# Two causal pooling layers: token means as TensorE products with a constant matrix, from token-major inputs in the first layer and from a token-major first product in the last

## The chip, the cores and the metric

The kernel runs on one core of one Trainium2 chip. The metric is the device time of one execution in microseconds (us). Times are the median of repeated runs; rows come from one execution that was recorded by the hardware profiler.

## The reference

One step of a decoder trunk with four layers on T = 264 tokens: a prompt of 256 new tokens, and 8 further sequences with one new token each and a state of their own. The model is 1024 wide. Layers 0 and 3 mix the tokens by pooling, layer 1 by a gated delta rule, layer 2 by retention, and a SwiGLU network (FFN) follows each. Every sublayer ends in a layer norm of `alpha * x + sublayer(x)`. The pooling mixer, cut to what matters:

```python
for gi, win in enumerate((2, 4, 8, 16)):       # four groups of 256 features
    lo, hi = gi * 256, (gi + 1) * 256
    s = c[:, 16:16 + T, lo:hi] - c[:, 16 - win:16 - win + T, lo:hi]   # c: running sum of [buffer, x]
    cnt = jnp.minimum(t + 1 + n_valid, win)
    means.append(s / cnt[None, :, None])
pooled = jnp.concatenate(means, axis=-1) - x
out = einsum('btgc,gcd->btgd', pooled by group, w) * scale
return out, ext[:, -15:]                        # and the last 15 input rows as the new state
```

For the 8 sample tokens the window reaches into `state_pool`, 15 earlier rows for each sequence.

## The kernel before

Activations lie feature-major: `x` is [128 partitions, 8 blocks, 264 tokens]. Every weight product is made of three fp32r products (`mm3`): both operands are split in a high part that fp32r holds exactly and the rest, and high by high, high by low and low by high are summed in PSUM. Weights come on SP's queue in 1 MB chunks (`raw`, a ring of three). ACT casts the high part in pieces of 128x512 (L205, `h`) and DVE subtracts it for the low part (L206, `l`); for the pooling weights POOL does the latter. So a chunk of weights needs a landing, casts on ACT and subtractions on DVE before TensorE can start with it.

A scheduler sets the order of the instructions, by its own model of their times, and each engine then runs its queue strictly in that order; `keep_in_program_order` pins single ones. An instruction that waits holds up all that stand behind it on its engine.

Layer norms of class `LN` come in two kinds. A deferred one hands its successor the unnormalised `d` times the gain, split in `zh` and `zl`. The next product is made from these, and mean and scale are put in later, when its results leave PSUM (`unfold`); x itself is made along the way by `apply`. One that is not deferred ends with `stats` and `finish`: sums on TensorE against a constant 1/1024, then mean `mr`, variance `vv`, `r` = 1/sqrt by Ln and Exp on ACT (L364, L365) and a Newton step on DVE (L366 to L368), then x by blocks. In before, the norm behind FFN 2 is of the second kind.

A pooling layer (`pool_layer`) takes x and makes the window sums by doubling shifts: adds of 128x510 elements and the like on DVE, for the group of window 16 on POOL (L545 to L560), and copies of the edges on ACT. `ph` and `pl` are the halves of the result (L561, L562) for 12 products per block of 128 outputs. L571 adds the product to `ax`, which is alpha times x. The mean `c` of the first two blocks (L331) is subtracted from all blocks before they are summed (L297, and on POOL L565 for groups 1 to 3). `busy` issues bf16 products with a constant tile `ob` that compute nothing; `BUSY` holds how many.

In an FFN the gate phase makes 22 pairs of products with `w13`, each followed by Silu on ACT (L456), a product on DVE (L457, `s`) and the split `gh` (L458) and `gl`. The down phase reads `w2` in chunks of 16 products, 11 chunks. Ahead of it a table of functions with Ln and Exp is loaded in ACT (L477), since Silu has another one. During FFN 2 the retention states are brought up to date: `st` and `vbc` are loaded, 1 MB each, and `out_ret_s` stored.

Of the kernel before, what the change touches and what calls it, by code (L numbers as in the profile page):

```python
# [19 lines left out]
P = 128  # L20
# [16 lines left out]

BUSY = ((20, 4), (44, 4))

# [21 lines left out]
CL, CN = _const_layout()  # L61
VL, VN = {}, 0
for _n, _c in (("psc", 16), ("lng", 64), ("lnb", 64), ("ng", 1), ("cw", 96), ("alog", 8), ("dtb", 8), ("corr", 128)):
    VL[_n] = (VN, _c)
    VN += _c


def make_consts():
# [33 lines left out]
    for h in range(H):  # L102
# [4 lines left out]
        dec[h, :, TP:] = d0[:, :P]  # L107
    return c.astype(np.float32), rope.astype(np.float32), dec.astype(np.float32), lev


@with_exitstack
def body(ctx: ExitStack, tc: tile.TileContext, ap):
# [156 lines left out]
    class LN:  # L269
# [5 lines left out]

        def __init__(self, idx, defer, on_pe=False):
            self.idx, self.defer, self.on_pe = idx, defer, on_pe
            self.c, self.seen = None, []
            self.d = pers.tile([P, KB, T], F32, tag="d", name=nm("d"))
            if on_pe:  # L280
                self.p1, self.p2 = sm_ps([P, T]), sm_ps([P, T])
            else:
                self.s1 = lnp.tile([P, T], F32, tag="s1", name=nm("s1"))
                self.s2 = lnp.tile([P, T], F32, tag="s2", name=nm("s2"))
            if defer:
                self.zh = pers.tile([P, KB, T + 2], F32R, tag="xz", name=nm("zh"), bufs=2)
                self.zl = pers.tile([P, KB, T + 2], F32R, tag="xz", name=nm("zl"), bufs=2)
                G.tensor_copy(self.zh[:, :, T:T + 2], gbh[:, idx])
                G.tensor_copy(self.zl[:, :, T:T + 2], gbl[:, idx])
# [53 lines left out]

        def stats(self):
            if self.on_pe:
# [40 lines left out]

        def apply(self, m):
# [5 lines left out]
            G.tensor_tensor(x[:, m], y, u, ADD)  # L393
            S.copy(xh[:, m], x[:, m])  # L394
            V.tensor_tensor(xl[:, m], x[:, m], xh[:, m].bitcast(F32), SUB)  # L395
# [51 lines left out]
    def ffn(l, pln):  # L447
        with tc.tile_pool(name=f"ffn{l}", bufs=1) as fp:
# [12 lines left out]
            for j in range(FB):  # L461
# [37 lines left out]

    def pool_layer(l, j, _):  # L500
        with tc.tile_pool(name=f"pool{l}", bufs=1) as pp:
            st = pp.tile([P, KB, NB, 15], F32, name=nm("st"))
            ob = pp.tile([P, 512], BF16, name=nm("ob"))
# [7 lines left out]
            busy(BUSY[l > 0][0])  # L511
            raw = wp.tile([P, CW], F32, tag="raw", name=nm("raw"))
            if l == 0:
                tc.keep_in_program_order(S.preload_act_table_set("natural_log_exp_and_others"))
            for g in range(4):
                w = slice(2 * g, 2 * g + 2)
                if l == 0:
                    nc.sync.dma_start(x[:, w], ap["xT"][:, w])
                    if g == 0:
                        nc.scalar.dma_start(vec, ap["vec"])  # L520
# [4 lines left out]
            if l == 0:  # L525
                small_loads()
            hl = [split(raw[:, i * 1024:(i + 1) * 1024], 1024, wp, "w", G) for i in range(2)]
            ss = pp.tile([P, KB, NB], F32, name=nm("ss"))
# [3 lines left out]
            co = W("corr", 0, 128).rearrange("p (b t) -> p b t", b=KB)  # L532
            ln = LN(l * 2, True, True)
            if l:
                tc.keep_in_program_order(S.preload_act_table_set("natural_log_exp_and_others"))
            for g in range(4):
                b0 = 2 * g
                win = 2 << g
                xb = x[:, b0:b0 + 2]
                E = G if g == 3 else V  # L540
                if g == 0:

                    dst = pp.tile([P, 2, T], F32, tag="s0", name=nm("sw"), bufs=2)
                    sc = 0.5
                    V.tensor_tensor(dst[:, :, 1:TP], xb[:, :, 0:TP - 1], xb[:, :, 1:TP], SUB)  # L545
                    G.tensor_tensor(dst[:, :, 0:1], xb[:, :, 0:1], xb[:, :, 0:1], SUB)
                    G.tensor_tensor(dst[:, :, TP:T], st[:, b0:b0 + 2, :, 14], xb[:, :, TP:T], SUB)
                else:
                    sc = 1.0
                    src = xb  # L550
                    for i in range(g + 1):
                        sh = 1 << i
                        dst = pp.tile([P, 2, T], F32, tag=f"s{g % 2}", name=nm("sw"), bufs=2)
                        E.tensor_tensor(dst[:, :, sh:TP], src[:, :, sh:TP], src[:, :, 0:TP - sh], ADD)
                        S.copy(dst[:, :, 0:sh], src[:, :, 0:sh])
# [20 lines left out]
                if g < 3:  # L576
                    busy(BUSY[l > 0][1])
            nc.scalar.dma_start(ap["pool_o"][j], st)
            tl = pp.tile([P, KB, 15 + NB], F32, name=nm("tl"))
            G.tensor_copy(tl, x[:, :, TP - 15:T])  # L580
            nc.scalar.dma_start(ap["pool_t"][j], tl)
            return ln
# [732 lines left out]
    "y": (P, KB, T),  # L1315
    "pool_o": (2, P, KB, NB, 15),
    "pool_t": (2, P, KB, 15 + NB),
# [9 lines left out]
def prepare(inp):  # L1327
# [24 lines left out]
    ch = lambda w: w.reshape(w.shape[:-1] + (w.shape[-1] // P, P))  # L1352
    corr = np.zeros((KB, 16))
    for b in range(KB):
        win = (2, 4, 8, 16)[b // 2]
        corr[b] = win / np.minimum(np.arange(16) + 1, win)
    vecs = [
# [6 lines left out]
        np.broadcast_to(a["gdn_dt_bias"][0], (P, 8)),  # L1364
        np.broadcast_to(corr.astype(np.float32).reshape(1, KB * 16), (P, KB * 16)),
    ]
    o["vec"] = con(np.concatenate(vecs, 1))
    o["cst"], o["rope"], o["rdec"], o["lev"] = make_consts()
    return o


def unpack(r):
    y = np.asarray(r["y"]).transpose(2, 1, 0).reshape(T, 1024)
    pt = np.asarray(r["pool_t"]).transpose(0, 3, 2, 1).reshape(2, 15 + NB, 1024)
    po = np.asarray(r["pool_o"]).transpose(0, 3, 4, 2, 1).reshape(2, NB, 15, 1024)
    pp = pt[:, None, :15]
# [27 lines left out]
```

## Time and profile before

| what | value |
|---|---|
| median of 3 runs | 1396.97 us (1396.32 to 1398.08) |
| the profiled execution's own time | 1399.02 us |
| its span, first to last instruction | 1397.2 us |
| mean granted TensorE clock | 0.978 of full speed |
| TensorE busy | 1326.9 us (95%) |
| VectorE (DVE) busy | 1044.3 us (75%) |
| ScalarE (ACT) busy | 841.8 us (60%) |
| GpSimd (POOL) busy | 460.2 us (33%) |

The time of the profiled execution lies 1.8 us above its span, and 2.05 us above the median of the other runs. TensorE's share is an average: it works without a break in the FFNs and waits at the two pooling layers and at a few other places.

### The profile page before, as it was taken

What the parts mean: (1) busy time and instruction counts of PE and PEld (TensorE: products, weight loads), DVE (VectorE), ACT (ScalarE), POOL (GpSimd) and SP (SyncE); (2) the same over time, 40 slices, a digit from 0 to 9 for tenths busy, and PEclk for the clock granted to TensorE, in tenths of its full rate; (3) what the DMA queues carried; (4) which work ended last, traced back from release to release, by engine and by line L of the source; (5) the groups of instructions that cost most, each with busy time, mean ns of one, the idle gap of its engine ahead of it and who ended that gap; (6) DMA issues with size and microseconds to landing.
All of it is one profiled execution on the core that took longest, in us unless ns stands there. A gap on an engine that the chain in (4) does not pass through costs nothing. (4 is left out here: it accounts for less than half of the span.)

```text
span 1397.2 us, 27688 instructions
## 1 busy us (share of the span) xinstructions
PE 1326.9 (95%) x10506; PEld 1273.5 (91%) x10509; DVE 1044.3 (75%) x2075; ACT 841.8 (60%) x1971; POOL 460.2 (33%) x518
## 2 busy tenths in 40 slices
PE   6999999879999999999979999999999998999996
PEld 4999999778998999999979999999998995999996
DVE  8885566989666799777697777668976758975564
ACT  4774544658564677675566665557765654774543
POOL 5230013563353443001278664133300144330022
PEclk8999999889999999999989999999999999999998
DMA  6355555421323355895645554456589961355550
GB/s 230 121 183 181 181 174 185 151 90 63 105 77 110 132 211 184 305 325 210 235 148 181 197 195 137 150 181 271 182 343 388 347 212 67 132 201 182 181 178 35
DMA packets 44341, 257.06 MB, mean 184 GB/s; under 512 B 5040, under 2 KB 9776, under 8 KB 16560
## 3 DMA queue, kind: packets, MB, share of 16 engines
q1 hardware_dynamic: 35936, 223.17, 44.9%
q10 hardware_dynamic: 5968, 19.55, 3.9%
q0 software_dynamic: 2304, 12.58, 2.2%
q8 instruction: 82, 1.34, 0.4%
q14 instruction: 51, 0.42, 0.1%
HBM read 238.45 MB, written 16.84 MB: 183 GB/s over the span
## 5 line engine op out<-in xcount | busy, mean ns | idle before, releaser
L206 DVE TENSOR_TENSOR l<-raw,h 128x512 fp32r<-128x512 f32 x658 | 463.1, 739 | 121.7 <-ACT h L205 116.9
L205 ACT CAST h<-raw 128x512 fp32r<-128x512 f32 x680 | 386.9, 616 | 193.9 <-PE mm L123 155.5
L123 PE MATMUL mm<-xh,h 128*128 128x264 f32 x1216 | 348.1, 288 | 8.2 <-ACT xh L394 4.0
L123 PE MATMUL mm<-xl,h 128*128 128x264 f32 x1216 | 348.4, 287 | 5.1 <-DVE xl L395 5.1
L123 PE MATMUL mm<-xh,l 128*128 128x264 f32 x1216 | 346.3, 287 | 0.0
L123 PEld LDWEIGHTS mm<-xh,h 128*128 128x128 f32 x1216 | 230.1, 190 | 10.8 <-ACT xh L394 4.8
L123 PEld LDWEIGHTS mm<-xl,h 128*128 128x128 f32 x1216 | 230.4, 189 | 5.9 <-DVE xl L395 5.3
L123 PEld LDWEIGHTS mm<-xh,l 128*128 128x128 f32 x1216 | 229.4, 189 | 0.7 <-DVE l L206 0.4
L123 PE MATMUL mm<-gh,l 128*128 128x264 f32 x704 | 199.6, 285 | 0.6 <-DVE l L206 0.6
L123 PE MATMUL mm<-gh,h 128*128 128x264 f32 x704 | 200.0, 284 | 0.0
L123 PE MATMUL mm<-gl,h 128*128 128x264 f32 x704 | 198.9, 283 | 0.0
L123 PE MATMUL mm<-zh,l 128*128 128x266 f32 x496 | 140.9, 289 | 3.0 <-DVE l L206 2.9
L123 PE MATMUL mm<-zh,h 128*128 128x266 f32 x496 | 142.1, 291 | 0.9 <-DVE ab L403 0.6
L123 PE MATMUL mm<-zl,h 128*128 128x266 f32 x496 | 142.5, 289 | 0.0
L123 PEld LDWEIGHTS mm<-gh,l 128*128 128x128 f32 x704 | 132.1, 188 | 1.0 <-DVE l L206 0.9
L123 PEld LDWEIGHTS mm<-gh,h 128*128 128x128 f32 x704 | 132.5, 188 | 0.1
L123 PEld LDWEIGHTS mm<-gl,h 128*128 128x128 f32 x704 | 132.5, 188 | 0.0
L404 POOL TENSOR_TENSOR ab<-ab,u 128x264 f32<-128x264 f32 x68 | 66.7, 992 | 138.5 <-DVE ab L403 59.6
L123 PE MATMUL mm<-xh,w 128*128 128x264 f32 x416 | 107.9, 314 | 2.1 <-DVE ab L403 2.1
L123 PEld LDWEIGHTS mm<-zh,l 128*128 128x128 f32 x496 | 92.9, 189 | 4.4 <-DVE l L206 4.1
L123 PEld LDWEIGHTS mm<-zh,h 128*128 128x128 f32 x496 | 93.1, 189 | 2.5 <-DVE ab L403 2.0
L123 PEld LDWEIGHTS mm<-zl,h 128*128 128x128 f32 x496 | 93.9, 189 | 1.0 <-DVE zl L300 0.2
(401 smaller groups left out, 2699.8 us busy)
## 6 DMA issues: line engine op xcount, KB each, us to landing
raw<-in_w_dram SPq DMA_DIRECT2D x132, 1024.0 KB
raw<-in_rwi_dram SPq DMA_DIRECT2D x24, 1024.0 KB
raw<-in_gwi_dram SPq DMA_DIRECT2D x16, 1024.0 KB
st<-in_rst_dram ACTq DMA_DIRECT2D x8, 1024.0 KB
raw<-in_rwo_dram SPq DMA_DIRECT2D x8, 1024.0 KB
st<-in_rst_dram SPq DMA_DIRECT2D x8, 1024.0 KB
vbc<-vdr SPq DMA_DIRECT2D x8, 1024.0 KB
out_ret_s_dram<-st POOLq DMA_DIRECT2D x8, 1024.0 KB, 10.6
```

The costliest lines, as they stand in the source:

```text
L123: i = nc.tensor.matmul(*a, **k)
L205: S.copy(hi[:, w], src_ap[:, w])
L206: (E or V).tensor_tensor(lo[:, w], src_ap[:, w], hi[:, w].bitcast(F32), SUB)
L404: (E or G).tensor_tensor(out, out, u[:n], ADD)
```

## The change

- **Layer 0.** Two new inputs: `xk`, the tokens of x and the pool state, token-major, 4 groups of [128, 3, 256] (393 KB each), and `pa`, constant matrices of means (128 x 4 x 296, 606 KB). `means` makes window mean minus x of one block by four fp32 products of 128, 16, 128 and 8 columns. The shifted adds, their edge copies and the correction table `corr` go away. `ph` and `pl` are made per block from PSUM. The pool state is stored from `xk` in four pieces, and no longer loaded as `st` (480 KB).
- **FFN 2.** The norm behind it is now deferred. `zh` and `zl` get 8 more columns, for the sums of the pool state of layer 3, which `pool_rows` loads ahead of `w2` in a slot of the ring `raw`.
- **Layer 3.** `pool_late` multiplies `zh` and `zl` with the pooling weights first, with tokens as the output's partitions (72 products of up to 256 columns into `zt` and `z3p`; four bf16 products with `zero` clear the banks). The statistics of the norm come behind that, a product with `m18` puts the mean in, `r` is turned to a column (`rc`), `zs` is `zt` times it, and `means` then makes the feature-major block. x is made by `apply` (L414 to L417 in the changed kernel). No `busy` and no load of a table are placed here.

```diff
-BUSY = ((20, 4), (44, 4))
+BUSY = (20, 4)
...
-            ln = LN(l * 2 + 1, l in (0, 1))
+            ln = LN(l * 2 + 1, l < DEPTH - 1, more=NB if l == 2 else 0)
+            if l == 2:
+                pool_rows(ln)
             tc.keep_in_program_order(S.preload_act_table_set("natural_log_exp_and_others"))
...
+    def pool_rows(ln):
+        st = wp.tile([P, CW], F32, tag="raw", name=nm("raw"))[:, 0:KB * NB * 15].rearrange("p (k b r) -> p k b r", k=KB, b=NB)
+        nc.sync.dma_start(st, ap["pst"])
+        nc.gpsimd.dma_start(ap["pool_o"], st)
...
+    def means(ps, rows, g, pa, n, o):
+        r0, r1, r2 = rows
+        PE.matmul(ps[:, P:TP], r1, pa[:, g, P:TP], start=True, stop=False)
+        PE.matmul(ps[:, P:P + 16], r0, pa[:, g, TP:TP + 16], start=False, stop=True)
+        PE.matmul(ps[:, 0:P], r0, pa[:, g, 0:P], start=True, stop=True)
+        PE.matmul(ps[:, TP:T], r2, o, start=True, stop=True)
...
+    def pool_late(l, j, pln):
...
+            for g in range(4):
...
+                PE.matmul(zt[g], zero[:, 0:P], zero, start=True, stop=False)
+                for c in (2, 0, 1):
...
+                    for kk in range(2):
+                        a, b = pln.zh[:, 2 * g + kk, w], pln.zl[:, 2 * g + kk, w]
+                        f = slice(kk * 256, kk * 256 + 256)
+                        PE.matmul(out, a, hi[:, f], start=c == 2 and kk == 0, stop=False)
+                        PE.matmul(out, b, hi[:, f], start=False, stop=False)
+                        PE.matmul(out, a, lo[:, f], start=False, stop=kk == 1 and c == 2)
+                S.copy(z3s[:, g], z3p[g // 2][:18, g % 2])
+            pln.stats(pa[:18, 3, 288:289])
...
+                for c in range(2):
+                    S.mul(zs[:, c], zt[g][:, c], rc[:, c:c + 1])
+                for m in (b0, b0 + 1):
+                    pln.apply(m, False)
...
+                    means(ps, (zs[:, 0, f], zs[:, 1, f], z3s[:, g, f]), g, pa, 18, a3[:, g])
+                    V.scalar_tensor_tensor(ln.d[:, m], ps[:, 0:T], W("psc", j * 8 + m), ax[:, m], MUL, ADD)
...
             for g in range(4):
-                nc.sync.dma_start(st[:, w], ap["pst"][j, :, w])
+                nc.sync.dma_start(xk[g], ap["xk"][g])
+                nc.scalar.dma_start(pa[:, g], ap["pa"][:, g])
...
+                    means(ps, (xk[g][:, 0, f], xk[g][:, 1, f], xk[g][:, 2, f]), g, pa, P, pa[:, g, 272:280])
+                    S.copy(ph[:, m], ps[:, 0:T])
+                    V.tensor_tensor(pl[:, m], ps[:, 0:T], ph[:, m].bitcast(F32), SUB)
...
+            for g in range(4):
+                nc.scalar.dma_start(ap["pool_k"][g], xk[g][:NB * 15, 2])
```

Three places in the order of the queues. The first is the head of ACT's queue, before; `raw_117` holds the pooling weights, and a wait names the semaphore that must have risen (DMAHW is a DMA).

```order
3 L524 DMA raw_117<-in_pw_dram 128x1024 x2
4 L170 DMA cst<-in_cst_dram 128x656
5 L174 DMA wba<-in_gba_dram 128x128 [waits DMAHW1_49]
6 L205 CAST h_143<-raw_117 128x512 [waits DMAHW3_49]
7 L205 CAST h_143<-raw_117 128x512
```

The same place of the changed kernel, where `raw_116` holds the pooling weights and `xk_119` to `xk_122` the four groups of `xk`:

```order
5 L645 DMA pa_118<-in_pa_dram 128x296
6 L645 DMA pa_118<-in_pa_dram 128x296 [waits DMAHW1_49]
7 L648 DMA raw_116<-in_pw_dram 128x1024 [waits DMAHW3_49]
8 L645 DMA pa_118<-in_pa_dram 128x296 [waits DMAHW5_49]
9 L191 DMA cst<-in_cst_dram 128x656 [waits DMAHW7_49]
10 L195 DMA wba<-in_gba_dram 128x128 [waits DMAHW0_49]
11 L226 CAST h_151<-raw_116 128x512 x2
```

The first cast has moved behind seven issues of transfers that each wait for an earlier one; DMAHW0 in row 10 is the landing of the third `xk`.

The second is ACT's queue where FFN 2 goes from its gate to its down phase, before. The last `s` is the Silu of the last gate pair, `raw_2227_14294` the first chunk of `w2`.

```order
1528 L205 CAST h_2228_14296<-raw_2227_14294 128x512 [waits DMAHW6_49,PE_49,Activation_49]
1529 L205 CAST h_2228_14296<-raw_2227_14294 128x512
1530 L205 CAST h_2230_14302<-raw_2227_14294 128x512 [waits DVE_49,PE_49]
1531 L205 CAST h_2230_14302<-raw_2227_14294 128x512
1532 L456 ACTIVATE s_2223_14278<-mm_2221_14228 128x264 [waits PE_49]
1533 L458 CAST gh_1961_12464<-s_2223_14278 128x264 [waits DVE_49]
```

The same place of the changed kernel, where `raw_2232_14323` is the first chunk of `w2`:

```order
1528 L538 CAST zh_2228_14308<-ss_2231_14315 128x8x8 [waits DVE_49]
1529 L505 ACT_TABLE_LOAD
1530 L482 ACT_TABLE_LOAD [waits PE_49]
1531 L482 ACTIVATE s_2224_14293<-mm_2222_14243 128x264 [waits Activation_49]
1532 L484 CAST gh_1962_12479<-s_2224_14293 128x264 [waits DVE_49]
1533 L226 CAST h_2233_14325<-raw_2232_14323 128x512 [waits DMAHW7_49]
```

The casts of the first chunk of `w2` have moved from ahead of the last Silu to behind it, and two loads of tables stand ahead of that Silu; in before the only one (L477) came 17 rows later.

The third is ACT's queue in layer 3 of the changed kernel, around the statistics of the norm (`sm_15208` is the sum of d):

```order
1612 L226 CAST h_15538<-raw_15536 128x512 [waits DMAHW0_49,PE_49,Pool_49]
1613 L226 CAST h_15538<-raw_15536 128x512
1614 L376 COPY mr_15212<-sm_15208 128x264 [waits PE_49]
1615 L381 ACTIVATE t_15216<-sm_15208 128x264
1616 L388 ACT_TABLE_LOAD
1617 L388 ACTIVATE r_15220<-vv_15218 128x264 [waits DVE_49]
1618 L389 ACT_TABLE_LOAD
1619 L389 ACTIVATE r_15220<-r_15220 128x264 [waits Activation_49]
```

In before the one load of this place (L535) stood ahead of the last products of FFN 2; now a load stands ahead of Ln and another ahead of Exp.

## Rows read from the trace of the kernel before

**Rows 1.** The page: busy us of each engine, share of the span, instructions.

```profile
PE 1326.9 (95%) x10506; PEld 1273.5 (91%) x10509; DVE 1044.3 (75%) x2075; ACT 841.8 (60%) x1971; POOL 460.2 (33%) x518
```

**Rows 2.** Busy time by engine, clock and DMA, three stretches of layer 0.

```profile
core 0: us, PE busy (x) PEld busy (x) DVE busy (x) ACT busy (x) POOL busy (x), PEclk, DMA share, GB/s
0.00:4.00 4.00, 2.53 (x6) 0.89 (x7) 0.56 (x2) 1.28 (x1) 0.19 (x4) 1.00 0.56 160
4.00:8.00 4.00, 3.79 (x15) 1.43 (x13) 1.30 (x6) 1.67 (x4) 2.43 (x6) 1.00 1.01 370
8.00:12.00 4.00, 1.92 (x12) 1.56 (x12) 3.99 (x7) 3.22 (x10) 4.00 (x5) 1.00 1.08 410
```

**Rows 3.** Timeline of layer 0, rows of ACT, DVE, POOL and PE (start, duration, instruction).

```profile
6.33 1.14 ACT L205 CAST h<-raw 128x512 fp32r<-128x512 f32 x2 [4.33 <-DMA raw<-in_pw_dram]
18.53 0.39 ACT L331 ACTIVATE c<-sm 128x264 f32<-128x264 f32 x1 [1.06 <-PE sm L123]
...
18.96 1.90 DVE L297 TENSOR_TENSOR d<-d,c 128x264 f32<-128x264 f32 x2
27.63 0.48 DVE L300 SCALAR_TENSOR_TENSOR zl<-d,vec,zh 128x264 fp32r<-128x264 f32 x1
28.03 1.28 DVE L206 TENSOR_TENSOR l<-raw,h 128x512 fp32r<-128x512 f32 x2
...
19.00 4.75 POOL L565 TENSOR_TENSOR ax<-ax,c 128x528 f32<-128x528 f32 x3 [2.02 <-ACT c L331]
...
35.30 0.60 PE L123 MATMUL mm<-ph,h 128*128 128x264 f32 x2
35.73 0.28 PE L123 MATMUL mm<-zh,h 128*128 128x266 f32 x1
35.85 0.29 PE L123 MATMUL mm<-zl,h 128*128 128x266 f32 x1
```

**Rows 4.** Timeline of ACT where FFN 2 turns from gate to down phase.

```profile
1082.32 0.39 ACT L456 ACTIVATE s<-mm 128x264 f32<-128x264 f32 x1 [1.56 <-PE mm L123]
1083.22 0.41 ACT L458 CAST gh<-s 128x264 fp32r<-128x264 f32 x1 [0.51 <-DVE s L457]
1083.54 1.14 ACT L205 CAST h<-raw 128x512 fp32r<-128x512 f32 x2
```

**Rows 5.** Timeline of ACT in FFN 3: a load of a table and the Silu behind it.

```profile
1199.84 1.28 ACT L456 ACT_TABLE_LOAD   x1
1201.13 0.43 ACT L456 ACTIVATE s<-ab 128x264 f32<-128x264 f32 x1
```

**Rows 6.** Timeline of PE in FFN 2: its longest wait there.

```profile
1057.52 0.39 PE L123 MATMUL mm<-xh,h 128*128 128x264 f32 x1 [2.64 <-ACT h L205]
```

**Rows 7.** Busy time, clock and DMA after that wait, and after one in layer 2.

```profile
1056.00:1058.00 2.00, 0.48 (x4) 0.48 (x4) 1.44 (x4) 1.47 (x4) 0.53 (x1) 1.00 1.00 422
...
720.00:722.00 2.00, 0.00 (x0) 0.00 (x0) 2.00 (x2) 1.94 (x6) 2.00 (x3) 1.00 0.00 0
728.00:732.00 4.00, 4.00 (x20) 4.00 (x20) 2.98 (x8) 0.69 (x2) 1.30 (x2) 0.50 0.27 53
```

**Rows 8.** Timeline from the end of FFN 2 to FFN 3, rows of four engines.

```profile
1147.95 1.05 PE L123 MATMUL sm<-s,cst 128*128 128x264 f32 x4
1148.84 0.61 PE L123 MATMUL sm<-d,cst 128*128 128x264 f32 x2
1150.61 9.44 PE L123 MATMUL sm<-ob 128*128 128x512 bf16 x43 [0.35 <-DMA st<-in_pst_dram]
...
1149.48 0.38 ACT L355 COPY mr<-sm 128x264 f32<-128x264 f32 x1
...
1155.08 0.86 DVE L368 SCALAR_TENSOR_TENSOR r<-t,r 128x264 f32<-128x264 f32 x1
...
1166.24 0.39 ACT L331 ACTIVATE c<-sm 128x264 f32<-128x264 f32 x1 [2.10 <-PE sm L123]
...
1182.94 0.59 PE L123 MATMUL mm<-ph,h 128*128 128x264 f32 x2
```

More of the change, by code (lines that the diff above doesn't have):

```diff
@@ L61 @@
 CL, CN = _const_layout()
+NPA = 296
 VL, VN = {}, 0
-for _n, _c in (("psc", 16), ("lng", 64), ("lnb", 64), ("ng", 1), ("cw", 96), ("alog", 8), ("dtb", 8), ("corr", 128)):
+for _n, _c in (("psc", 16), ("lng", 64), ("lnb", 64), ("ng", 1), ("cw", 96), ("alog", 8), ("dtb", 8)):
     VL[_n] = (VN, _c)
@@ L107, in make_consts @@
         dec[h, :, TP:] = d0[:, :P]
-    return c.astype(np.float32), rope.astype(np.float32), dec.astype(np.float32), lev
+    pa = np.zeros((P, 4, NPA))
+    for w in range(4):
+        win = 2 << w
+        d = i[None, :] - i[:, None]
+        on = (d >= 0) & (d < win)
+        pa[:, w, 0:128] = on / np.minimum(i[None, :] + 1, win) - np.eye(P)
+        pa[:, w, 128:256] = on / win - np.eye(P)
+        d = 128 + np.arange(16)[None, :] - i[:, None]
+        pa[:, w, 256:272] = (d < win) / win
+        for b in range(NB):
+            pa[b * 15 + 16 - win:b * 15 + 15, w, 272 + b] = 1.0 / win
+            pa[NB * 15 + b, w, 272 + b] = 1.0 / win - 1.0
+            pa[10 + b, w, 280 + b] = 1.0 / win
+    for b in range(NB):
+        pa[b, 0, 288 + b] = 1.0
+        pa[8, 1, 288 + b] = 1.0
+        pa[9, 2, 288 + b] = 1.0
+    pa[8, 3, 288] = 1.0
+    return pa.astype(np.float32), c.astype(np.float32), rope.astype(np.float32), dec.astype(np.float32), lev
 @with_exitstack
@@ L269, in body, with __init__ @@
     class LN:
-        def __init__(self, idx, defer, on_pe=False):
+        def __init__(self, idx, defer, on_pe=False, more=0):
             self.idx, self.defer, self.on_pe = idx, defer, on_pe
@@ L285, in __init__ @@
             if defer:
-                self.zh = pers.tile([P, KB, T + 2], F32R, tag="xz", name=nm("zh"), bufs=2)
-                self.zl = pers.tile([P, KB, T + 2], F32R, tag="xz", name=nm("zl"), bufs=2)
+                self.zh = pers.tile([P, KB, T + 2 + more], F32R, tag="xz", name=nm("zh"), bufs=2)
+                self.zl = pers.tile([P, KB, T + 2 + more], F32R, tag="xz", name=nm("zl"), bufs=2)
                 G.tensor_copy(self.zh[:, :, T:T + 2], gbh[:, idx])
@@ L355, in stats @@
             S.copy(mr, p1)
+            if sel is not None:
+                self.m18 = lnp.tile([18, T], F32, tag="m18", name=nm("m18"))
+                V.tensor_scalar(self.m18, mr[:18], sel, None, MUL)
             t = lnp.tile([P, T], F32, tag="t", name=nm("t"))
@@ L385, in finish, with apply @@
                 S.activation(x[:, m], y, AF.Identity, bias=bm)
-        def apply(self, m):
+        def apply(self, m, parts=True):
             u = lnp.tile([P, T], F32, tag="u", name=nm("u"), bufs=2)
@@ L393, in apply @@
             G.tensor_tensor(x[:, m], y, u, ADD)
+            if not parts:
+                return
             S.copy(xh[:, m], x[:, m])
@@ L498, in ffn @@
             return ln
-    def pool_layer(l, j, _):
-        with tc.tile_pool(name=f"pool{l}", bufs=1) as pp:
-            st = pp.tile([P, KB, NB, 15], F32, name=nm("st"))
+    def pool_rows(ln):
+        st = wp.tile([P, CW], F32, tag="raw", name=nm("raw"))[:, 0:KB * NB * 15].rearrange("p (k b r) -> p k b r", k=KB, b=NB)
+        nc.sync.dma_start(st, ap["pst"])
+        nc.gpsimd.dma_start(ap["pool_o"], st)
+        ss = lnp.tile([P, KB, NB], F32, tag="ss", name=nm("ss"))
+        for g in range(4):
+            w = slice(2 * g, 2 * g + 2)
+            V.tensor_reduce(ss[:, w], st[:, w, :, 16 - (2 << g):15], AX.X, ADD)
+        zh, zl = (z[:, :, T + 2:T + 2 + NB] for z in (ln.zh, ln.zl))
+        S.copy(zh, ss)
+        V.tensor_tensor(zl, ss, zh.bitcast(F32), SUB)
@@ new lines, in means, with pool_tail @@
+    def means(ps, rows, g, pa, n, o):
[4 more added lines that the diff above has]
+        PE.matmul(ps[:, TP:T], r2, o, start=True, stop=True)
+    def pool_tail(pp, j):
+        tl = pp.tile([P, KB, 15 + NB], F32, name=nm("tl"))
+        G.tensor_copy(tl, x[:, :, TP - 15:T])
+        nc.scalar.dma_start(ap["pool_t"][j], tl)
@@ L503, in pool_layer @@
+    def pool_layer(l, j, pln):
+        if pln is not None:
+            return pool_late(l, j, pln)
+        with tc.tile_pool(name=f"pool{l}", bufs=1) as pp:
             ob = pp.tile([P, 512], BF16, name=nm("ob"))
@@ L509, in busy @@
                     tc.keep_in_program_order(PE.matmul(pob, ob[:, 0:P], ob, start=True, stop=True))
-            busy(BUSY[l > 0][0])
+            busy(BUSY[0])
             raw = wp.tile([P, CW], F32, tag="raw", name=nm("raw"))
-            if l == 0:
-                tc.keep_in_program_order(S.preload_act_table_set("natural_log_exp_and_others"))
+            tc.keep_in_program_order(S.preload_act_table_set("natural_log_exp_and_others"))
+            pa = pp.tile([P, 4, NPA], F32, name=nm("pa"))
+            xk = [pp.tile([P, 3, 256], F32, name=nm("xk")) for _ in range(4)]
+            nc.scalar.dma_start(vec, ap["vec"])
             for g in range(4):
[L516 to L520, printed above, removed]
-                nc.sync.dma_start(st[:, w], ap["pst"][j, :, w])
+                nc.sync.dma_start(xk[g], ap["xk"][g])
+                nc.scalar.dma_start(pa[:, g], ap["pa"][:, g])
                 if g % 2 == 0:
@@ L524, in pool_layer @@
                     nc.scalar.dma_start(raw[:, h], ap["pw"][j, :, h])
[L525 to L526 removed]
+                w = slice(2 * g, 2 * g + 2)
+                nc.sync.dma_start(x[:, w], ap["xT"][:, w])
+            small_loads()
             hl = [split(raw[:, i * 1024:(i + 1) * 1024], 1024, wp, "w", G) for i in range(2)]
[L528 removed]
             ph = pp.tile([P, KB, T], F32R, name=nm("ph"))
@@ L564, in pool_layer @@
+                for e in range(2):
+                    m = b0 + e
+                    f = slice(e * P, e * P + P)
+                    ps = mm_ps()
+                    means(ps, (xk[g][:, 0, f], xk[g][:, 1, f], xk[g][:, 2, f]), g, pa, P, pa[:, g, 272:280])
+                    S.copy(ph[:, m], ps[:, 0:T])
+                    V.tensor_tensor(pl[:, m], ps[:, 0:T], ph[:, m].bitcast(F32), SUB)
+                S.mul(ax[:, b0:b0 + 2], x[:, b0:b0 + 2], ALPHA)
                 if g:
@@ L576, in pool_layer @@
                 if g < 3:
[L577 to L581, printed above, removed]
+                    busy(BUSY[1])
+            for g in range(4):
+                nc.scalar.dma_start(ap["pool_k"][g], xk[g][:NB * 15, 2])
+            pool_tail(pp, j)
             return ln
@@ L1315 @@
     "y": (P, KB, T),
-    "pool_o": (2, P, KB, NB, 15),
+    "pool_k": (4, NB * 15, 256),
+    "pool_o": (P, KB, NB, 15),
     "pool_t": (2, P, KB, 15 + NB),
@@ L1352, in prepare @@
     ch = lambda w: w.reshape(w.shape[:-1] + (w.shape[-1] // P, P))
[L1353 to L1356, printed above, removed]
     vecs = [
```

90 lines of the change are left out of this document (57 added, 33 removed).

## The prediction

> **What bounds the kernel now.** I read the page first: TensorE is busy for 1326.9 of 1397.2 us and DVE for 1044.3 [rows 1], so time is made or lost only where TensorE waits. Then the windows and timelines of the three places that the change touches.
>
> In layer 0 the loads fill the DMA engines (share 1.01 to 1.08) and DVE works without a gap from 8 us on (3.99 of 4.00 us), while TensorE works less than half of its time [rows 2]. The weights land at 6.33, the mean `c` is out at 18.53, and the first products of FFN 0 start at 35.73 [rows 3]. They run ahead there: two `ph` products started at 35.30, and ten more products of the pooling layer and four sums of the norm come later between those of FFN 0. At a step of 0.12 us for a product [rows 3] and 0.445 for a sum (four records, which are two sums, from 1147.95 to 1148.84 [rows 8]) that is 12 x 0.12 + 4 x 0.445 = 3.2 us. So FFN 0 starts, all counted, at 35.30 + 3.2 = 38.5.
>
> The same sum for layer 3: FFN 2's last product is followed by the sums of the norm at 1147.95, which I call T0. `r` is there at 1155.08 + 0.86 = 1155.94 (T0 + 8.0), `c` at 1166.24 (10.3 later), the last pooling products start at 1182.94 (16.7 later) [rows 8], and 3.2 us are left over: T0 + 38.2. TensorE spends 9.44 us of this on 43 products that compute nothing [rows 8].
>
> In FFN 2 TensorE is the bound and waits seldom; its longest wait is 2.64 us for casts on ACT [rows 6]. At the turn to the down phase it does not wait, because the first chunk of `w2` is cast before the last Silu, as the order of ACT's queue shows.
>
> **The change, layer 0.** The shifted adds leave DVE; `pl` per block enters at about the 0.48 us of a `zl` [rows 3]. But the first cast now stands behind issues that wait for transfers. Up to the third `xk` and what goes beside it, 3.44 MB must land (3 x 393 KB of `xk`, 2 x 264 KB of x, 606 KB of `pa`, 1 MB of weights, 0.13 MB of `vec`). Rows 2 give 4 x 160 + 4 x 370 GB/s = 2.1 MB by 8 us and 410 GB/s then: 8 + 1.3 / 0.41 = 11.3, and some 0.4 for the issue: ACT starts at 11.7 and not at 6.33. From there I walk through the queues: first block's means and cast at about 15, the second group's at 18.7, `c` between 21.5 (means of 0.75 us) and 24.6 (at the half clock), 3 to 6 us later than before. Behind `c` DVE carries what is left: two subtractions of `c` (1.90 in the row beside POOL), some two `pl`, six `d` and eight `zl` at about 0.48, four casts' low parts at 0.64 [rows 3], together 1.9 + 7.7 + 2.6 = 12.2 us, against the 16.8 that passed before from 18.53 to 35.30. So the layer ends at 33.7 to 36.8, with about 1.3 us of its work left on TensorE: 35.0 to 38.1. I take 36.0, a gain of 2.5. The four products of `means` in fp32 do not occur before; by columns, 280 against 264, one block lies at or above a sum's 0.445, and as small products cost more I take 0.75 to 1.0. If `c` were not late at all, the layer would end at 18.5 + 12.2 + 1.3 = 32.0, a gain of 6.5; with `c` at 24.6 and DVE slowed by POOL it loses 1.
>
> **The change, FFN 2.** On ACT the last Silu now waits for TensorE's last gate product behind a load of a table that waits for the same, and the casts of the first `w2` chunk stand behind it. In the rows the Silu starts at 1082.32 and the next cast behind `gh` at 1083.54, 1.22 later [rows 4]; a load takes 1.28 [rows 5]. So the first half of the cast starts 1.28 + 1.22 = 2.5 us after the last gate product, takes 0.57, and TensorE can begin; its second product wants the low part, another 0.5 to 0.64 on DVE. I count 2.5 + 0.57 + 0.5 = **3.6 us** of waiting where there was none. TensorE is the bound behind it, so nothing gives it back. Nothing excludes that it is more: the state's 0.49 MB is read and written again in a stretch whose DMA engines are full (422 GB/s at a share of 1.00 [rows 7]), which is 2.3 us of them, and `w2` comes behind it on SP's queue; by my walk it lands just in time, and costs up to 4 us if not. The sums for the deferred norm (one more `zh` and `zl` per block, about 0.5 us each on ACT and DVE) lie under a down phase in which TensorE needs 66 products, 8 us, for each block: nothing. If that cover were gone it would be some 8 us.
>
> **The change, layer 3.** Behind T0 TensorE now has 16 small and 48 large products, 4 that clear banks and 8 others, at about 0.12 to 0.22 each some 9.6 us; the sums stand behind them, at T0 + 9.65 to 10.55. On ACT `mr` and `t` take 0.7, then come load, Ln, load, Exp (2 x 1.28 + 2 x 0.42) where both loads were hidden before, then three steps on DVE: `r` at T0 + 16.5 instead of 8.0. From `r` to `c`: `rc` waits on DVE behind a `y` that waits for POOL, `zs` follows at T0 + 20.4, the first `d` stands behind eight `y` and comes at 25.0, `c` at 28.0: 11.5 against 10.3. From `c` on nothing but POOL's `ax` minus `c` (4.75 us for three [rows 3]) and the last blocks' `d`, square and sums: 9.4 against 16.7, and six sums, 2.7 us, are left. 16.5 + 11.5 + 9.4 + 2.7 = T0 + 40.1, a loss of **1.9**. Means of 0.75 us and faster `y` make it a gain of 2; the half clock a loss of 6. FFN 3 has two more loads in its first statistics, 2.6 us; its third and fourth products wait for PSUM some 5 us later, which covers them. Without that cover they cost 2.6.
>
> The sum against the profiled execution: 1399.02 - 2.5 + 3.6 + 1.9 = 1402.0. That execution lay 2.05 above the median, so I forecast **1400.0**. A difference under 0.2%, 2.8 us, can't be told from none; mine is at that border.
>
> The table loads are where a rule weighs more than a row. Here the load is over at 1199.84 + 1.28 = 1201.12 and the Silu starts at 1201.13 [rows 5]: a switch costs its 1.28. The Trainium skill, "ScalarE: Activation LUTs", section "What ACT_TABLE_LOAD costs", adds a drain of about 1380 ns to each load. This trace disagrees with an added 1380 ns at that place, where ACT had just been at work.
>
> **The rivals.**
>
> *The clock falls* (0.20). After a stretch in which TensorE did nothing (720 to 722) the granted clock was 0.50 and still so at 728 to 732, with TensorE busy throughout, so at the lower level of 1.2 GHz and about 4 us lost; after the wait of 2.64 us it stayed at 1.00 [rows 6, 7]. My wait of 3.6 lies between, and in layer 3 TensorE has some 4 us without work before `zs`, with no `ob` products to fill them. One drop costs 4, two with the fp32 products of layer 3 at half speed 8: 1404 to 1408.
>
> *Layer 0 pays in full and layer 3 does too* (0.27): the other side. The mechanism is DVE's relief: if `c` is not held back by the landings, layer 0 gives 6.5, and a layer 3 without adds gives 2, against 3.6 in FFN 2: 1397 - 4.9 = 1392. It decides from the point where `c` comes before 20 us. For it speaks that DVE is full for all of layer 0; against it that 1.6 MB more come ahead of `c`.
>
> *The gains cancel* (0.15): layer 0 gives about 4, the wait in FFN 2 3.6, layer 3 nothing: 1396 to 1398.
>
> *Each load on the path costs twice as much* (0.05): three loads now lie on it (the Silu's, and those before Ln and Exp); if ACT waited 1.3 us more at each, the sum would be 3.9 higher, 1403.9. The row of FFN 3 speaks against it [rows 5].
>
> **How the numbers follow.** My forecast has 0.33, with a range of its own of 1397.5 to 1402.5, half of it within the border. The range of 8 in 10 reaches from the full gains to one or two drops of the clock: 1391 to 1407. Faster: 0.27 and a little of the cancelling case, 0.29. Same: 0.15 and almost half of mine, 0.29. Slower: 0.42.
>
> **What would show it.** After: ACT's first cast at 11 to 12; `c` at 21 to 25; FFN 0's products without a break from 34 to 36. A wait of TensorE of 3 to 4 us between the last gate and the first down product of FFN 2, ended by ACT's `h` or DVE's `l`, with two loads of tables before the last Silu. In layer 3 `r` 16 to 17 us after the last product of FFN 2, and FFN 3's products from 36 to 38. I am wrong if that first wait is not there, if `c` of layer 0 comes before 20, or if the clock stays at 0.5 for long behind these waits.

## The result, and the profile after

The changed kernel took 1414.15 us in the median against 1396.64 before, a ratio of 1.011 (95% interval 1.0093 to 1.0127): it is slower, by 1% or a little more. One of its four executions, the recorded one, ran at a granted clock of 0.744 from end to end, took 1628.99 us and is left out of the ratio. Measured again, the kernel took 1415.54 against 1395.99, a ratio of 1.0134 (1.0117 to 1.0151). The rows of the changed kernel below come from an execution of this second measurement, of 1416.12 us.

From the page of the changed kernel, its span, its busy times and the granted clock in 40 slices:

```profile
span 1414.3 us, 27882 instructions
PE 1345.4 (95%) x10625; PEld 1297.8 (92%) x10625; DVE 1023.4 (72%) x2066; ACT 852.1 (60%) x1978; POOL 440.0 (31%) x509
PEclk8999999889999999999999999999999996999998
```

DVE is 21 us less busy than in [rows 1], and TensorE 18.5 us more. The work left DVE as the change says, and TensorE, the engine that was busy for 95% of the time already, took it. A part of its 18.5 us is no new work but the lower clock in layer 3, and against it stand the 43 products of [rows 8], 9.44 us, that are gone. The 34th slice of the clock, which is layer 3, has fallen to 6.

Where the 17.1 us between the two spans came about is read from three marks on TensorE. The last gate product of FFN 2 starts at 1081.63, and started at 1082.37 before: nothing is lost up to there. The last product of FFN 2's down phase starts at 1151.42 (1147.83 before): 4.3 us are lost in the down phase. All the rest, 13.5 us, is lost between that product and the end. FFN 3 itself is no longer: from its first Silu to its last it takes 116.9 us in both kernels (1218.2 to 1335.1, 1201.1 to 1318.0). So layer 3, with FFN 3's beginning up to that first Silu, took the 13.5.

**FFN 2's turn.** ACT and then TensorE in the timeline of the changed kernel; they answer to [rows 4]:

```profile
1081.62 1.28 ACT L482 ACT_TABLE_LOAD   x1 [2.54 <-PE mm L144]
1082.92 0.39 ACT L482 ACTIVATE s<-mm 128x264 f32<-128x264 f32 x1
1083.81 0.41 ACT L484 CAST gh<-s 128x264 fp32r<-128x264 f32 x1 [0.50 <-DVE s L483]
1084.12 2.18 ACT L226 CAST h<-raw 128x512 fp32r<-128x512 f32 x4
...
1084.79 0.39 PE L144 MATMUL mm<-gh,h 128*128 128x264 f32 x1 [2.87 <-ACT h L226]
1085.52 0.39 PE L144 MATMUL mm<-gh,l 128*128 128x264 f32 x1 [0.22 <-DVE l L227]
```

The order was read rightly: load, Silu, `gh`, and only then the cast of the first chunk of `w2`, 2.50 us after the load began. TensorE waits 2.87 and 0.22 us. Behind the wait the granted clock falls too, as the windows show:

```profile
1084.00:1086.00 2.00, 0.99 (x6) 0.79 (x7) 1.66 (x4) 2.00 (x5) 0.00 (x0) 1.00 0.99 418
1086.00:1088.00 2.00, 2.00 (x14) 2.00 (x13) 2.00 (x6) 2.00 (x5) 0.00 (x0) 0.64 0.65 274
1088.00:1090.00 2.00, 2.00 (x11) 2.00 (x11) 2.00 (x7) 1.70 (x4) 0.00 (x0) 0.51 0.88 242
1090.00:1092.00 2.00, 2.00 (x18) 2.00 (x18) 2.00 (x5) 2.00 (x5) 0.53 (x1) 1.00 0.98 406
```

With TensorE busy for all of 1086 to 1090, a clock of 0.64 and 0.51 costs 2 x 0.36 + 2 x 0.49 = 1.7 us. Together 4.8; a wait of 0.65 us for `l` that stood at 1095 before is gone.

**Layer 3.** TensorE in the timeline (the first row is the norm's sums, `mm<-z3s,m` are the products with `m18`, `mm<-pa,zs` and `mm<-a,z3s` together the means of one block):

```profile
1162.30 1.05 PE L144 MATMUL sm<-s,cst 128*128 128x264 f32 x4
1164.67 3.72 PE L144 MATMUL mm<-z3s,m 18*128 18x256 f32 x16 [1.33 <-DVE m L379]
1169.05 1.01 PE L144 MATMUL sm<-cst,r 1*128 1x1 f32 x4 [0.66 <-DVE r L392]
1173.67 1.65 PE L144 MATMUL mm<-pa,zs 128*128 128x128 f32 x6 [3.61 <-ACT zs L606]
1175.25 0.59 PE L144 MATMUL mm<-a,z3s 18*128 18x8 f32 x2
1175.77 1.65 PE L144 MATMUL mm<-pa,zs 128*128 128x128 f32 x6
...
1198.90 0.48 PE L144 MATMUL mm<-zh,h 128*128 128x266 f32 x1
```

The last row is FFN 3's first product. On ACT, the first load of a table behind the sums, with what stands before and behind it, and `c`:

```profile
1163.73 0.39 ACT L381 ACTIVATE t<-sm 128x264 f32<-128x264 f32 x1
1164.14 1.28 ACT L388 ACT_TABLE_LOAD   x1
1165.44 0.42 ACT L388 ACTIVATE r<-vv 128x264 f32<-128x264 f32 x1
...
1182.83 0.39 ACT L352 ACTIVATE c<-sm 128x264 f32<-128x264 f32 x1 [3.27 <-PE sm L144]
```

The same stretch by engine, with the clock behind the five busy times:

```profile
1162.00:1166.00 4.00, 2.67 (x14) 2.04 (x14) 1.89 (x4) 3.53 (x7) 0.39 (x2) 1.00 0.49 205
1166.00:1170.00 4.00, 3.34 (x16) 2.63 (x14) 2.27 (x7) 2.09 (x3) 0.00 (x0) 0.81 0.00 0
1170.00:1174.00 4.00, 0.39 (x2) 0.34 (x2) 3.26 (x12) 3.54 (x9) 2.64 (x4) 0.50 0.00 0
1174.00:1182.00 8.00, 7.37 (x27) 6.35 (x27) 3.48 (x6) 4.90 (x10) 4.19 (x7) 0.50 0.04 13
1182.00:1190.00 8.00, 8.00 (x26) 6.57 (x26) 6.40 (x10) 4.54 (x11) 4.45 (x3) 0.50 0.01 2
1190.00:1198.00 8.00, 8.00 (x34) 6.71 (x32) 1.48 (x3) 1.83 (x5) 0.00 (x0) 0.64 0.00 0
```

This is the reading on which everything hangs. From 1182 on TensorE does not wait at all, and DVE, which was full in this layer before, is idle for most of the time from 1190. So TensorE is the bound of layer 3 now, and it runs at the lower level of 1.2 GHz for most of 1170 to 1198. One block's means take 2.10 us (1173.67 to 1175.77), and from the first means to FFN 3's first product it is 25.2 us.

**Layer 0.** ACT's first cast and `c`, which answer to the first rows of [rows 3]:

```profile
11.51 1.14 ACT L226 CAST h<-raw 128x512 fp32r<-128x512 f32 x2 [9.50 <-DMA pa<-in_pa_dram]
23.01 0.39 ACT L352 ACTIVATE c<-sm 128x264 f32<-128x264 f32 x1 [1.73 <-PE sm L144]
```

Both came where the prediction put them, some 5 us later than before. Behind `c` TensorE is the fuller engine, busy for 11.82 of 12 us against DVE's 10.63:

```profile
24.00:28.00 4.00, 3.93 (x26) 3.32 (x26) 4.00 (x6) 3.54 (x10) 3.96 (x3) 1.00 0.00 1
28.00:32.00 4.00, 3.89 (x26) 3.08 (x25) 4.00 (x8) 2.57 (x7) 0.55 (x1) 1.00 0.63 180
32.00:36.00 4.00, 4.00 (x28) 3.30 (x26) 2.63 (x7) 1.93 (x5) 0.00 (x0) 1.00 0.83 344
```

The first Silu of FFN 0 starts at 54.9 and started at 53.6: no gain is left.

### The profile page after: what moved, and what is told of

Read it like the earlier page. It is cut to its first block, busy times and chain, and to the rows that moved or that the text cites. A ratio compares the mean times of both kernels' runs of the same rounds, so it can differ in the third digit from the quotient of the medians.

```text
span 1627.2 us, 27882 instructions
## 1 busy us (share of the span) xinstructions
PE 1583.7 (97%) x10625; PEld 1529.0 (94%) x10625; DVE 1023.6 (63%) x2066; ACT 861.5 (53%) x1978; POOL 427.7 (26%) x509
## 3 DMA queue, kind: packets, MB, share of 16 engines
q1 hardware_dynamic: 35792, 225.91, 40.1%
## 4 chain that ended last, share of the span: by engine, by line
PE 92%; DVE 4%; ACT 2%; issue 1%; DMA 1%; POOL 1%; ACTq 0%; DVEq 0%; POOLq 0%
PE mm L144 78%; PE sm L144 12%; PE sm L149 2%; DMA raw<-in_pw_dram 0%; DVE l L227 0%; DVE lm L956 0%; DVE y L416 0%; DMA pa<-in_pa_dram 0%; ACT junk L904 0%; ACT h L226 0%; ACT w L252 0%; ACT x L409 0%; DVE qk L1262 0%; DVE xl L421 0%; DVE t L391 0%
## 5 line engine op out<-in xcount | busy, mean ns | idle before, releaser
L144 PE MATMUL mm<-xh,h 128*128 128x264 f32 x1216 | 387.1, 321 | 3.7 <-ACT h L226 2.2
L144 PE MATMUL mm<-xl,h 128*128 128x264 f32 x1216 | 388.0, 320 | 2.5 <-DVE xl L421 2.5
L144 PE MATMUL mm<-xh,l 128*128 128x264 f32 x1216 | 385.8, 320 | 0.0
L144 PEld LDWEIGHTS mm<-xh,h 128*128 128x128 f32 x1216 | 251.1, 207 | 5.1 <-ACT h L226 2.7
L144 PEld LDWEIGHTS mm<-xl,h 128*128 128x128 f32 x1216 | 252.1, 207 | 3.2 <-DVE xl L421 2.8
L144 PEld LDWEIGHTS mm<-xh,l 128*128 128x128 f32 x1216 | 251.4, 208 | 0.5
L144 PE MATMUL mm<-gh,h 128*128 128x264 f32 x704 | 224.2, 319 | 2.8 <-ACT h L226 2.8
L144 PE MATMUL mm<-gl,h 128*128 128x264 f32 x704 | 225.0, 320 | 0.0
L144 PE MATMUL mm<-gh,l 128*128 128x264 f32 x704 | 224.2, 320 | 0.2 <-DVE l L227 0.2
L144 PE MATMUL mm<-zh,l 128*128 128x266 f32 x496 | 158.0, 323 | 0.0
```

The source lines that it names most:

```text
L144: i = nc.tensor.matmul(*a, **k)
```

## The experiments

Theory A: the loss sits in FFN 2's turn and in layer 3. Theory B: the changed kernel gets a lower clock over the whole execution. The second time given for a run is that of the kernel before, timed beside it on the same chip; ratios are to that.

**The changed kernel again.**

> The changed kernel itself, timed again, for a trace at the usual clock. Theory A (the loss is in places: FFN 2's turn and layer 3): about 1411 us; TensorE waits 3 to 4 us at FFN 2's turn, and from the last product of FFN 2 to FFN 3, all leftover work counted, it takes 45 to 50 us where it took 38.2, because the eight fp32 products with m18 and the products of the means cost some 0.5 to 0.7 and 1.5 to 2 us and the clock falls there; layer 0 within 2 us of before. Theory B (the changed kernel gets a lower clock over the whole execution): granted clock under 1.00 in stretches of the FFNs, where nothing was changed.

1415.54 against 1395.99. In windows of 8 us over the whole trace the clock is 1.00 in the FFNs but for the stretch behind the turn. Theory B is out for this execution. Theory A has the places right and the size of layer 3 too small: 51.7 us, leftover work counted, and not 45 to 50.

**Layer 0 alone.** FFN 2 and layer 3 are those of before:

```diff
-            ln = LN(l * 2 + 1, l < DEPTH - 1, more=NB if l == 2 else 0)
-            if l == 2:
-                pool_rows(ln)
+            ln = LN(l * 2 + 1, l in (0, 1))
...
-            return pool_late(l, j, pln)
+            return pool_mid(l, j)
```

`pool_mid` holds the pooling layer of the kernel before.

> Layer 0 of the change alone; FFN 2 and layer 3 as before. Theory A: 1395 to 1399 us, no difference from before that can be measured. Theory B: 1400 or more, a part of the loss, since the products with the constant matrices are there. By the prediction's term for layer 0 alone: 1394.5.

1397.68 against 1395.99, 1.0006 (0.9995 to 1.0016): no difference, as theory A has it.

**FFN 2 and layer 3 alone.** Layer 0 is that of before:

```diff
     def pool_layer(l, j, pln):
         if pln is not None:
             return pool_late(l, j, pln)
+        (the body of the kernel before)
```

> FFN 2 and layer 3 of the change alone; layer 0 as before. Theory A: 1408 to 1414 us, nearly the whole loss. Theory B: between before and the changed kernel, near 1402 to 1405. By the prediction's terms for these two places: 1402.5.

1414.95 against 1395.99, 1.0135 (1.0119 to 1.0152): the whole loss, and 12 us more than the prediction's terms for these two places.

**FFN 2's turn mended.**

```diff
-            if l == 2:
-                pool_rows(ln)
-            tc.keep_in_program_order(S.preload_act_table_set("natural_log_exp_and_others"))
+            if l != 2:
+                tc.keep_in_program_order(S.preload_act_table_set("natural_log_exp_and_others"))
...
                 if k == FB - 1:
                     resid(ln, m, ps[:, 0:T])
+                    if l == 2 and m == 5:
+                        pool_rows(ln)
```

> The changed kernel with FFN 2's turn mended: the pool state is loaded after the sixth block of the down phase and the load of a table ahead of the down phase is left out, by which the casts of the first w2 chunk come ahead of the last Silu again. Theory A: 3 to 4 us less than the changed kernel in the same call, and no wait at the turn. If the wait also costs the clock (the prediction's rival): 6 to 8 less. Theory B: no less.

1413.56 against 1395.99, 1.0123 (1.0106 to 1.014), 2.0 us less than the changed kernel beside it, with intervals that overlap: less than theory A's 3 to 4, and none of the 6 to 8. In the trace the turn is mended: the down phase starts without a wait and lasts from 1081.73 to 1147.11,

```profile
1081.55 0.39 ACT L482 ACTIVATE s<-mm 128x264 f32<-128x264 f32 x1 [1.56 <-PE mm L144]
1082.46 0.41 ACT L484 CAST gh<-s 128x264 fp32r<-128x264 f32 x1 [0.51 <-DVE s L483]
```

so its last product comes 4.3 us earlier. Only 2.8 us of that are left at the end of the span (1411.5 against 1414.3); the rest was lost again in layer 3, where the clock fell earlier (0.54 from 1162 to 1164), the products with `m18` took 5.75 us in place of 3.72, and the first means began 24.4 us behind FFN 2's last product and not 22.1. The turn's price is shown there, but not in the whole to better than some 2 us.

**The clock in layer 3.** Two runs with bf16 products that compute nothing, in the manner of `busy`; the second has two more behind each product with `m18`:

```diff
-                PE.matmul(prc[:, c:c + 1], pln.r[0:1, c * P:c * P + P], ones[0:1, 0:1], start=True, stop=True)
+                tc.keep_in_program_order(PE.matmul(prc[:, c:c + 1], pln.r[0:1, c * P:c * P + P], ones[0:1, 0:1], start=True, stop=True))
+            G.tensor_copy(obr, pln.r)
+            warm(obr, 34)
```

> The changed kernel with 34 bf16 products that compute nothing behind the turn of r to a column, until zs is there (they read a bf16 copy of r that POOL makes, so that they can't start earlier). Theory C (the 3.6 us in which TensorE waits for zs bring the clock down, and the half clock costs 12 of the 17 us): clock 1.00 from zs on, 1402 to 1406 us. Theory D (the clock falls for the stretch from the sums on, in which TensorE runs eight fp32 products with only 18 rows, between gaps): the clock still falls before r, and is back earlier than now; 1405 to 1411. Theory E (the fp32 products of the means are the cost at any clock): no gain of more than 4.

> As the run before, and two such products (of a bf16 copy of mr) behind each of the eight fp32 products with m18. Theory C: no more than the run before. Theory D: the clock stays at 1.00 throughout layer 3, 1402 to 1406 us. Theory E: no gain of more than 4 over the changed kernel.

The first took 1408.56 against 1397.68, 1.0085 (1.0069 to 1.0101), the second 1412.35, 1.0119 (1.0103 to 1.0135). In the first the clock still falls before `r`, and is back by the time the means begin:

```profile
1166.00:1170.00 4.00, 3.42 (x16) 2.65 (x17) 3.83 (x14) 2.30 (x5) 2.23 (x3) 0.50 0.00 0
1170.00:1174.00 4.00, 4.00 (x25) 2.97 (x24) 2.71 (x7) 4.00 (x10) 2.80 (x4) 0.65 0.01 2
1174.00:1182.00 8.00, 7.91 (x53) 6.87 (x51) 4.86 (x9) 5.57 (x14) 5.43 (x7) 1.00 0.05 14
...
1173.90 0.83 PE L144 MATMUL mm<-pa,zs 128*128 128x128 f32 x6
1174.66 0.38 PE L144 MATMUL mm<-a,z3s 18*128 18x8 f32 x2
1174.97 0.94 PE L144 MATMUL mm<-pa,zs 128*128 128x128 f32 x6
...
1188.19 0.48 PE L144 MATMUL mm<-zh,h 128*128 128x266 f32 x1
```

One block's means now take 1.07 us (1173.90 to 1174.97) and not 2.10: the same products at the other level. From the first means to FFN 3's first product it is 14.3 us and not 25.2 (one sum fewer is done by then). The run gained 7 us by the ratios (1.0134 to 1.0085), although its 34 products lasted until 1173.90 and the means began 2.7 us later behind FFN 2's last product; the recorded execution is its fastest, 1405.76. So it is the clock and not the fp32 products as such, and theory D is right in that the clock falls before the turn of `r`, without the long wait for `zs`. In the second run the fillers behind `m18` did not keep it up, against theory D: it was 0.51 and 0.50 from 1166 to 1178, and the fillers themselves, at that clock, put off `r`'s turn to a column to 1173.28.

**Before, without its fillers.** `BUSY` of layer 3 set to (0, 0).

> The kernel before without its 43 products and 12 further ones that compute nothing in layer 3. If what the change loses there is the clock that these held up: the granted clock falls to 0.50 in layer 3 for more than the two short stretches of before, and the time rises by 3 to 8 us, less than in the changed kernel, since DVE is the bound there. If they do nothing: 1396 to 1398.

1398.14 against 1397.68, 1.0004 (0.9995 to 1.0014): nothing, though the clock does fall. My expectation of 3 to 8 us was wrong, and the reason is the counterpart of the reading above:

```profile
1152.00:1160.00 8.00, 0.00 (x0) 0.00 (x0) 7.06 (x12) 4.30 (x10) 7.02 (x10) 0.53 0.45 168
1160.00:1168.00 8.00, 6.97 (x22) 5.36 (x23) 7.47 (x14) 5.05 (x16) 3.56 (x4) 0.50 0.04 12
1168.00:1176.00 8.00, 6.73 (x33) 5.33 (x32) 8.00 (x8) 4.37 (x11) 7.64 (x6) 0.90 0.00 0
```

TensorE is at the lower level for some 16 us here (some 6 with the fillers), for the first 8 of them without work. But DVE is the full engine (7.06, 7.47, 8.00), and TensorE has slack. The fillers that the change dropped had been worth nothing; the slack that it used up had been worth something.

**One load of a table.** The table with both functions is loaded ahead of the statistics:

```diff
+            tc.keep_in_program_order(S.preload_act_table_set("natural_log_exp_and_others"))
             pln.stats(pa[:18, 3, 288:289])
```

> The changed kernel with one load of the table that has both Ln and Exp ahead of the norm's statistics in layer 3, so that the two loads behind the sums go away. r comes 2.6 us earlier. If the wait of TensorE is thereby too short for the clock to fall: 1403 to 1406; if not: 1412 to 1414, 1 to 3 us less than the changed kernel.

1411.30 against 1397.68, 1.0102 (1.0083 to 1.0122), some 4 us less than the changed kernel in ratio (1.0134 to 1.0102), between the two times expected and with intervals that overlap. In the trace, which is of its fastest execution (1407.55), the clock is at 0.50 from 1166 to 1186, some 20 us against 27 in the changed kernel (from 1169 to 1196). The first means come only 1.0 us earlier behind FFN 2's last product (21.1 and not 22.1), and from them to FFN 3's first product it takes 21.1 us and not 25.2: most of what layer 3 gained here came with the clock.

**Rows or gaps.** The products with `m18` over 128 rows, 110 of them zeros:

```diff
-                    PE.matmul(zt[g][:, c], pln.m18[:, c * P:c * P + P], z3s[:, g], start=False, stop=c == 1)
+                    PE.matmul(zt[g][:, c], m18w[:, c * P:c * P + P], z3w[:, g], start=False, stop=c == 1)
```

> The changed kernel with the eight products with m18 made over 128 rows, of which 110 hold zeros, in place of 18 rows; gaps and durations stay. If the clock falls because of the few rows: 1.00 at 1166 to 1170 us, and the fall, if any, comes only with the wait for zs; 1405 to 1412 us. If it falls because of the gaps around these products: the same clock and the same time as the changed kernel, 1412 to 1416.

1413.78 against 1397.77, 1.0117 (1.01 to 1.0134), and a clock of 1.00 from 1166 to 1170, 0.58 from 1170 to 1174. The fall came some 2 us later, only in the wait for `zs`, as the first reading has it; the time is the same within the intervals, as the second has it. That doesn't decide it.

**Layer 0's queue.** Layer 0 alone, with `pa`, the constants and the stores on POOL's queue:

```diff
-                nc.scalar.dma_start(pa[:, g], ap["pa"][:, g])
+                nc.gpsimd.dma_start(pa[:, g], ap["pa"][:, g])
```

> Layer 0 of the change alone, with the transfers of pa, the constants, wba and the stores of the pool state on POOL's queue, so that ACT's first cast waits for its own weights alone. If the late start of ACT is what holds layer 0 back (the prediction's step): c 3 to 5 us earlier and 1391 to 1395 us. If the landings and TensorE's fp32 products at the lower clock set the pace: c within 2 us of now, 1395 to 1399.

1402.04 against 1397.77, 1.0038 (1.0023 to 1.0053): slower. ACT's first cast came at 8.73 and not 11.51, but the scheduler now put the means of two more blocks, and the products of the blocks between, ahead of the sums for `c`, and `c` came at 27.28. Both are outside what was expected. TensorE, at 0.56 and 0.50 from 12 to 24 us, was busy from 13.51 on without a gap until `c`:

```profile
12.00:20.00 8.00, 6.49 (x30) 6.49 (x31) 2.23 (x5) 3.45 (x8) 4.81 (x8) 0.56 1.04 416
20.00:24.00 4.00, 4.00 (x20) 4.00 (x20) 0.87 (x2) 1.11 (x3) 0.00 (x0) 0.50 0.35 139
```

So here TensorE's own queue at the lower level held `c` back, and not ACT's start. What an earlier start of ACT gives with the order on TensorE unchanged is not shown: TensorE began with the pooling products only 1.1 us earlier (13.51 and not 14.61).

**All mended.** The turn and the one load as above, 12 fillers between the sums and `m18`, 24 behind `r`:

```diff
             pln.stats(pa[:18, 3, 288:289])
...
+            warm(obc, 12)
...
+            G.tensor_copy(obr, pln.r)
+            warm(obr, 24)
```

> The changed kernel with four things mended at once: FFN 2's turn as in the run for it, one load of the table for Ln and Exp ahead of the statistics, 12 bf16 products that compute nothing in the gap between the norm's sums and the first product with m18, and 24 behind the turn of r. By the runs so far: 3 to 5 us back at the turn, 2.6 from the loads, 8 to 12 from the clock in layer 3; 1397 to 1402 us, that is about as fast as before. If the clock falls in layer 3 in spite of the products: 1403 to 1408.

1402.26 against 1397.77, 1.0038 (1.0018 to 1.0057): about two thirds of the loss is back. Its eight executions lie near the two expected ranges: five at a mean clock of 0.981 to 0.984 took 1397.75 to 1402.32, three at 0.976 took 1405.94 to 1408.28. The recorded one is the slowest, and its clock still fell, though all but 0.30 us of the gap before `m18` is filled and TensorE works throughout 1166 to 1170; it came back and fell again from 1174 on:

```profile
1162.91 3.72 PE L144 MATMUL mm<-z3s,m 18*128 18x256 f32 x16 [0.30 <-DVE m L379]
...
1166.00:1170.00 4.00, 4.00 (x26) 3.13 (x26) 3.74 (x13) 3.31 (x8) 1.87 (x4) 0.74 0.00 0
1170.00:1174.00 4.00, 3.60 (x23) 2.90 (x21) 2.00 (x4) 3.53 (x8) 3.18 (x5) 0.84 0.01 2
1174.00:1182.00 8.00, 7.73 (x29) 6.57 (x29) 3.03 (x5) 3.96 (x9) 3.05 (x5) 0.55 0.05 14
1182.00:1190.00 8.00, 8.00 (x29) 6.69 (x29) 6.06 (x11) 2.72 (x7) 3.17 (x3) 0.60 0.00 0
```

No version was faster than the kernel before in the median.

## Why the prediction was wrong

The direction was right, the size was not: a loss of 3 was forecast, with a range of 1391 to 1407, and by the two medians 17.5 came, 19.6 when it was measured again.

*Layer 0, a gain of 2.5.* Mis-sized: layer 0 alone gave 1.0006, nothing. The chain up to `c` was right (ACT at 11.7, though 8 + 1.3 / 0.41 is 11.2 and not 11.3, measured 11.51; `c` at 21.5 to 24.6, measured 23.01). The step that failed is DVE's 12.2 us behind `c` as the only pace, with 1.3 us left on TensorE: the sums, the means of the last groups and the fillers share TensorE's queue, which was full from 24 to 36. FFN 0's first product came at 36.00, but six sums, four fillers and six pooling products were still to come behind it, some 4.1 us by the steps of the prediction.

*FFN 2's turn, a loss of 3.6.* Right: 3.1 us of waiting, and 4.3 over the down phase, the clock's 1.7 included. That the wait would also bring the clock down was a rival at 0.20, and it happened. The mechanism stands also by the run that mends the order.

*Layer 3, a loss of 1.9.* This is the term that failed; 13.5 were lost. Up to `r` the walk was nearly right (with T0 the first product behind FFN 2, 1151.54: sums at 10.8 and not 9.65 to 10.55, `r` at 17.5 and not 16.5); `c` came at 31.3 and not 28.0. The failing sentence is "From `c` on nothing but POOL's `ax` minus `c` (4.75 us for three [rows 3]) and the last blocks' `d`, square and sums: 9.4 against 16.7, and six sums, 2.7 us, are left." From `c` to FFN 3's first product it took 16.1 us and not 9.4. With the six sums that were left, and some 1.6 us by which FFN 3's beginning became longer (from its first product to its first Silu 19.3 and not 17.8, which the prediction put at nothing), that is T0 + 51.7 and not 40.1.

I asked only what DVE and POOL had to do there. TensorE has 8 x 1.07 us for the means and 12 sums at 0.445 ahead of FFN 3's first product, 13.9 us at the full clock. That is more than DVE's 11.4 from 1174 to 1198, and at half clock it is twice as much. From 1174 to 1198 the mean clock was (16 x 0.50 + 8 x 0.64) / 24 = 0.55, so 24 us held 13 of work: some 11 us, about what the forecast lacked in this term. The run with fillers behind `r` measures the same: 14.3 us in place of 25.2. At the full clock the walk comes out nearly right. In that run FFN 3's first Silu is at T0 + 58.6, against 66.7 in the changed kernel and 53.2 before, and of the 5.4 us that are still lost 2.7 are the later start of the means behind the fillers.

*The rivals.* The clock had 0.20 and 4 to 8 us, 1404 to 1408. It was the right mechanism with too small a price, because I counted the fall as a stretch that ends by itself (4 us) and not as one in which the engine with the most work stays at half speed, from 1169 to 1196. The prediction's own sign of being wrong, a clock that stays at 0.5 for long behind these waits, is what came. That the loads cost twice as much is refuted: in the changed kernel too the Silu starts at 1082.92, 1.30 after the load began at 1081.62, and Ln at 1165.44, 1.30 after its load, which began 0.02 after `t` was done. By the Trainium skill, "ScalarE: Activation LUTs", section "What ACT_TABLE_LOAD costs", a switch takes some 1.4 us more than the load; the trace disagrees here as in [rows 5].

What stays open: what exactly brings the clock down in layer 3. It fell during the products with `m18` or within some 2.4 us after them in every run with the late part, with and without fillers. In the changed kernel gaps of 1.33 and 0.66 us lie ahead of it, in the mended one a gap of 0.30 us, while a gap of 2.64 us in FFN 2 left it up [rows 6, 7]. So gaps alone do not account for it. With 18 rows the fall came some 1.5 to 5.0 us after the first of these products, depending on the run, and with 128 rows some 6.1 us after it; that doesn't decide whether the rows matter. And the turn's share in the whole is known only to some 2 us.

## What to carry to other kernels

When work moves from an engine that is full to TensorE, price it at the lower clock too, and ask whether TensorE stays under the other engines then: here 13.9 us of products took 25.2 in a stretch ahead of which TensorE had waited. Slack on TensorE is worth something even where it is filled with products that compute nothing; removing those cost nothing, using the slack cost some 11 us. And where a scheduler sets the order, a new instruction without dependencies (here a load of a table) can move ahead of one that waits, so look at what now stands behind it.

## What the hardware showed that was not expected

Some 16 us of a clock at 0.50 in layer 3 cost nothing in the kernel before (1398.14 without its fillers against 1397.68), and 27 us of it some 11 us in the changed one. Four fp32 products of 128, 16, 128 and 8 columns took 1.07 us at the full clock, where a product of 264 columns takes 0.445: small columns cost more than their number says. And two fillers between the products with `m18`, with TensorE busy almost without a gap from 1162.49 on, did not keep the clock from falling at 1166.
